# Modulation products of two 128-row blocks issued together, and seven raw tiles in place of four

## The chip, the core and the metric

The kernel runs on one core of a Trainium2 chip. Its engines work side by side: TensorE (PE; its weight loads are listed apart as PEld), VectorE (DVE), ScalarE (ACT), GpSimd (POOL) and SyncE (SP), which here only issues DMA transfers. The metric is device time in microseconds for one execution; the median of the runs counts, and less is better.

## The reference

Two layers of a trunk with 640 tokens of 1024 features (128 context tokens and 512 latent ones). Each layer has an FFN, a mixer and a second FFN. In front of each stands a norm with a shift and a scale, behind it a gate; the nine vectors of a layer come from the condition by one matrix product, the modulation, and this is what the change is about:

```
def adaln(cond, w, b):                       # w: (1024, 9 * 1024) for each layer
    m = (jax.nn.silu(cond) @ w + b).reshape(cond.shape[0], 1, N_MOD, D_MODEL)
    return [m[:, :, j] for j in range(N_MOD)]

for i in range(DEPTH):                       # DEPTH = 2; c_ctx for context, c for latent tokens
    m_ctx = adaln(c_ctx[None, :], mod_w[i], mod_b[i])
    m_lat = adaln(c, mod_w[i], mod_b[i])
    ...                                      # x += 1/2 gate * post(swiglu(pre(x) * (1 + scale) + shift)), and so on
```

Two condition vectors are multiplied with a matrix of 1024 x 9216 for each layer, 75 MB of weights in all, all in float32.

## The kernel before

**The modulation** is a generator, `adaln` (from L363 on). It works through groups (l, q): five for each layer, of 2048 columns each, the last of 1024. A group is the sum over eight blocks (`kc`) of 128 rows of the weights. For one block, `load` asks SP's DMA queue (L376) for two tiles `mw` of 128 x 1024 (one in the last group of a layer), and four matmuls follow (L393; two in a last group). The stationary operand is the 32-column `cT`, which holds the two conditions, the moving one 512 columns of weights; `tile_position=(0, 32 * j)` puts the four on four 32-column tiles of the array, so that they write four strips of one PSUM bank, `ad`. After each block the generator yields. At a group's end the bias `mb` is added (L399), and TensorE transposes the sum (L403).

**Who asks.** Outside, each call of `step()` or `filler()` runs the generator to its next yield: eight calls at the start, then one for each step `t` of an FFN (up to the number in `FILLS`), several at the end of an FFN behind its last products, and others between the pieces of the even mixer. With `self.look` set (in the mixer's scan and attention), a block's weights are asked for one call earlier.

**The raw tiles.** `raw()` gives one of four buffers of 128 x 1024 float32 (pool `rawp`), taken in turn as they come free. All weights land in them: the blocks `u` and `v` of an FFN step (L587) and the rows of its second matrix (L201), the mixers' projections (L196), the modulation's `mw` and `mb`, and the gates `gb`. A weight block is split in two parts by ScalarE and VectorE (`hi`, `lo`, L599 and L600), which frees its raw tile; an `mw` tile is read by TensorE itself, and its products free it.

**The FFN** forms its first product by seven products of halves (L646, 128 x 320 into `up`) and mixes them with pieces of the second (L298, 128 x 512 into `dn`). A step `t` handles 128 of 2816 hidden features. **The even mixer** projects (L208), runs a chunked scan (L1267 to L1287) and latent attention (keys and values from `ukv`, loaded at L1475 and first used at L1484; L1507 to L1580).

**What sets the order.** The code is written as one sequence; a scheduler gives each engine its own order of instructions from it, by their place in the sequence and by what they need. Each engine then works in that order. SP issues its transfers one after the other, and one that waits for a buffer holds up those behind it.

## Time and profile before

| | |
|---|---|
| median of 3 runs | 2749.08 us (2747.61 to 2754.76) |
| profiled execution, span from first to last instruction | 2748.3 us |
| TensorE, matmuls | 2671.1 us busy, 97% |
| TensorE, weight loads | 2335.4 us busy, 85% |
| VectorE | 1944.1 us busy, 71% |
| ScalarE | 1186.0 us busy, 43% |
| GpSimd | 125.5 us busy, 5% |
| DMA | 309.60 MB, mean 113 GB/s |

The profiled execution has no time of its own beside its span. An engine's busy share is a mean over stages. The matmuls are pipelined: one that is listed with 0.31 us may be followed by the next after 0.15, so what a matmul costs is read from one start to the next. The granted clock is given as a share of 2.4 GHz.

### The profile page before, as it was taken

How to read it: one execution, taken by the hardware profiler on the slowest of the kernel's cores; microseconds unless marked ns; L12 is line 12 of the kernel's file. 1: busy time of each engine (PE TensorE's matmuls, PEld its weight loads, DVE VectorE, ACT ScalarE, POOL GpSimd, SP SyncE). 2: the span in 40 equal slices, each digit the busy share in tenths (PEclk: the TensorE clock that was granted, in tenths of full speed). 3: DMA queues.
4: the chain of work that ended last, by engine and by line, in shares of the span. 5: the costliest groups of instructions: out<-in, count | busy, mean ns of one | idle time of the engine just before them, and what ended most of it. 6: DMA issues, size and time to landing. Idle time of an engine off the chain costs nothing.

```text
span 2748.3 us, 41207 instructions
## 1 busy us (share of the span) xinstructions
PE 2671.1 (97%) x16040; PEld 2335.4 (85%) x16040; DVE 1944.1 (71%) x3731; ACT 1186.0 (43%) x2285; POOL 125.5 (5%) x301
## 2 busy tenths in 40 slices
PE   6999999999999999999999999999999999999998
PEld 4888888788867678888997889999899988999997
DVE  5777677768575558667777777777775738777776
ACT  5433323555435556333335533333665446433333
POOL 0000000200100011000001000000200002000001
PEclk9999999999999999999999999999999999999999
DMA  7344333734141343434226432223312243322223
GB/s 251 116 125 142 124 115 106 236 113 124 57 157 57 118 161 116 129 115 131 77 70 195 131 96 84 85 70 112 125 43 73 64 133 115 93 85 85 74 80 123
DMA packets 297099, 309.60 MB, mean 113 GB/s; under 512 B 13573, under 2 KB 250639, under 8 KB 296903
## 3 DMA queue, kind: packets, MB, share of 16 engines
q1 hardware_dynamic: 278240, 260.05, 30.6%
q10 hardware_dynamic: 18663, 46.92, 4.9%
q8 instruction: 126, 2.06, 0.3%
q14 instruction: 70, 0.57, 0.1%
HBM read 286.59 MB, written 20.33 MB: 112 GB/s over the span
## 4 chain that ended last, share of the span: by engine, by line
PE 56%; issue 33%; DMA 3%; DVE 3%; ACT 2%; POOL 2%; POOLq 0%; DVEq 0%; ACTq 0%
PE up L646 18%; PE dn L298 13%; PE up L208 9%; PE ad L393 3%; PE up L1830 2%; PE dn L1810 1%; DMA mw<-in_mod_w_dram 1%; PE up L1542 1%; POOL rstd L231 1%; POOL ss L223 1%; POOL rstd L230 1%; DMA mb<-in_mod_b_dram 0%; DMA raw<-in_ffn_w_in_dram 0%; PE up L1575 0%; DMA cf<-const_cf_dram 0%
## 5 line engine op out<-in xcount | busy, mean ns | idle before, releaser
L646 PE MATMUL up<-ar,hi 128*128 128x320 f32 x2944 | 662.4, 313 | 8.6 <-ACT ar L509 3.9
L646 PEld LDWEIGHTS up<-ar,hi 128*128 128x128 f32 x2944 | 503.8, 189 | 40.5 <-ACT ar L509 5.5
L646 PE MATMUL up<-ar,lo 128*128 128x320 f32 x1472 | 457.0, 311 | 0.1
L599 ACT CAST hi<-raw 128x1024 fp32r<-128x1024 f32 x256 | 267.6, 1050 | 376.5 <-PE up L646 227.2
L600 DVE TENSOR_TENSOR lo<-raw,hi 128x1024 fp32r<-128x1024 f32 x256 | 312.6, 1222 | 89.6 <-ACT hi L599 88.9
L304 DVE TENSOR_TENSOR y<-y,dn 128x512 f32<-128x512 f32 x388 | 264.4, 683 | 147.7 <-PE dn L298 147.3
L298 PE MATMUL dn<-hi,al 128*128 128x512 f32 x880 | 347.1, 395 | 0.6 <-DVE al L687 0.6
L298 PE MATMUL dn<-hi,ah 128*128 128x512 f32 x880 | 346.7, 395 | 1.0 <-DVE y L304 0.9
L298 PE MATMUL dn<-lo,ah 128*128 128x512 f32 x880 | 347.5, 395 | 0.0
L646 PE MATMUL up<-hq,hi 128*128 128x320 f32 x1408 | 318.9, 312 | 0.0
L646 PEld LDWEIGHTS up<-ar,lo 128*128 128x128 f32 x1472 | 278.8, 189 | 1.7 <-issue 0.8
L646 PEld LDWEIGHTS up<-hq,hi 128*128 128x128 f32 x1408 | 238.4, 188 | 41.1 <-issue 22.6
L208 PE MATMUL up<-ar,hi 128*128 128x384 f32 (+1 forms) x1184 | 266.8, 315 | 4.5 <-ACT ar L274 3.7
L208 PEld LDWEIGHTS up<-ar,hi 128*128 128x128 f32 x1184 | 199.8, 190 | 21.2 <-issue 12.8
L646 PE MATMUL up<-hq,lo 128*128 128x320 f32 x704 | 217.5, 309 | 0.0
L183 DVE TENSOR_TENSOR lo<-raw,hi 128x1024 fp32r<-128x1024 f32 x145 | 176.0, 1219 | 51.0 <-ACT hi L182 47.2
L298 PEld LDWEIGHTS dn<-hi,al 128*128 128x128 f32 x880 | 165.4, 188 | 39.3 <-DVE al L687 1.3
L298 PEld LDWEIGHTS dn<-hi,ah 128*128 128x128 f32 x880 | 165.2, 188 | 25.2 <-DVE y L304 2.3
L208 PE MATMUL up<-ar,lo 128*128 128x384 f32 (+1 forms) x592 | 184.8, 312 | 0.0
L298 PEld LDWEIGHTS dn<-lo,ah 128*128 128x128 f32 x880 | 165.3, 188 | 22.4
L182 ACT CAST hi<-raw 128x1024 fp32r<-128x1024 f32 x145 | 151.3, 1048 | 42.4 <-PE up L646 15.1
L646 PE MATMUL up<-hq,hilo 128*128 128x320 f32 x960 | 155.5, 310 | 0.0
(704 smaller groups left out, 4139.3 us busy)
## 6 DMA issues: line engine op xcount, KB each, us to landing
raw<-in_ffn_w_in_dram SPq DMA_DIRECT2D x188, 512.0 KB
mw<-in_mod_w_dram SPq DMA_DIRECT2D x144, 512.0 KB
raw<-in_ffn_w_out_dram SPq DMA_DIRECT2D x88, 512.0 KB
xdr<-x ACTq DMA_DIRECT2D x25, 512.0 KB
x<-xdr ACTq DMA_DIRECT2D x25, 512.0 KB
raw<-in_od_w_in_dram SPq DMA_DIRECT2D x24, 512.0 KB
raw<-in_ev_w_in_dram SPq DMA_DIRECT2D x19, 512.0 KB
gb<-gate ACTq DMA_DIRECT2D x12, 512.0 KB
```

Source lines behind the costliest of these rows:

```text
L182: nc.scalar.copy(hi, raw)
L183: nc.vector.tensor_sub(lo, raw, hi.bitcast(F32))
L208: self.nc.tensor.matmul(ps[:, :n], lhsT=wt[a][:, kc], rhs=self.h[g][:, b, kc], start=k == 0, stop=k == 3 * KC - 1)
L223: nc.gpsimd.tensor_tensor(s2, tot, ss, ALU.add)
L230: nc.gpsimd.tensor_scalar(r, ss, 1.0 / D, EPS, ALU.mult, ALU.add)
L298: nc.tensor.matmul(ps, lhsT=a(i, m), rhs=w[j][:, nh * 512:nh * 512 + 512], start=k == 0, stop=k == last)
L304: nc.vector.tensor_add(yd, yd, ps)
L393: nc.tensor.matmul(ps[32 * j:32 * j + 32, :], lhsT=self.cT[:, kc], rhs=wt[j // 2][:, (j % 2) * 512:(j % 2) * 512 + 512], start=kc == 0, st ...
L599: nc.scalar.copy(hi, raw[:, :n])
L600: nc.vector.tensor_sub(lo, raw[:, :n], hi.bitcast(F32))
L646: nc.tensor.matmul(ps[:, :HT], lhsT=w[i][:, kc], rhs=b[j].at(kc), start=first and n == 0, stop=n == 11, skip_group_check=not first)
L1830: nc.tensor.matmul(ps[:, :256], lhsT=T.ht(a, kc, m), rhs=ws[kc // 4][b][:, kc % 4], start=k == 0, stop=k == 23)
```

## The change

Nothing is left out or added in what is computed. The code changes in three places; all docstrings and comments are gone too, and lines below L393 stand two to four lines further down (L646 is L650 after, L393 is L395).

```
-        self.rawp = mk("rawp", 4)
+        self.rawp = mk("rawp", 7)
...
                 ps = self.ps_ad.tile([P, 512], F32, tag="ad", name=self.u("ad"))
+                held = []
                 for kc in range(KC):
                     if not ready:
                         load()
-                    wt = ready.pop(0)
+                    held.append((kc, ready.pop(0)))
                     if self.look:
                         load()
-                    for j in range(nj):
-                        nc.tensor.matmul(ps[32 * j:32 * j + 32, :], lhsT=self.cT[:, kc], rhs=wt[j // 2][:, (j % 2) * 512:(j % 2) * 512 + 512], start=kc == 0, stop=kc == KC - 1, tile_position=(0, 32 * j))
+                    one = (l, q) == (0, 0)
+                    for k, wt, j in [(k, wt, j) for k, wt in held for j in range(nj)] if one or kc % 2 else []:
+                        nc.tensor.matmul(ps[32 * j:32 * j + 32, :], lhsT=self.cT[:, k], rhs=wt[j // 2][:, (j % 2) * 512:(j % 2) * 512 + 512], start=k == 0, stop=k == KC - 1, tile_position=(0, 32 * j))
+                    if one or kc % 2:
+                        held = []
                     if kc < KC - 1:
                         yield False
...
-    nc = bacc.Bacc("TRN2", target_bir_lowering=False, num_devices=1)
+    nc = bacc.Bacc("TRN2", target_bir_lowering=False, num_devices=1, dynamic_dma_scratch_size=1024)
```

In the first group the blocks' products are issued one block at a time, as before. In all others a call with even `kc` only asks for the block's weights and keeps them; the call with odd `kc` issues the products of both blocks. A kept block holds its raw tiles for one call longer. The pool of raw tiles grows by three, 12 KB in each partition, and the scratch space for DMA descriptors shrinks to make room.

Where the instructions stand is shown at three places. The first is TensorE's order in the first FFN, for the first two blocks of the second group of layer 0; `ad` is the modulation's bank, `mw` a weight tile with its number, `up` and `dn` the FFN's products. Before, the first block stands behind a piece of the second product:

```order
L298 MATMUL dn_2429<-lo_2266,ah_2237 128x512
L298 MATMUL dn_2429<-hi_2265,al_2238 128x512
L393 MATMUL ad_2457<-mw_2458,cT 32x512 x2
L393 MATMUL ad_2457<-mw_2460,cT 32x512 x2
L646 MATMUL up_2474<-hq_784,hi_2446 128x320
```

and the second block one step later, in two pieces:

```order
L646 MATMUL up_2496<-ar_403,lo_2447 128x320
L393 MATMUL ad_2457<-mw_2644,cT 32x512 x2
L646 MATMUL up_2660<-hq_784,hi_2621 128x320
L646 MATMUL up_2660<-hq_785,hi_2621 128x320
L646 MATMUL up_2660<-hq_784,lo_2622 128x320
L646 MATMUL up_2660<-hq_784,hi_2621 128x320
L646 MATMUL up_2660<-hq_785,hi_2621 128x320
L646 MATMUL up_2660<-hq_784,lo_2622 128x320
L646 MATMUL up_2660<-hq_784,hi_2621 128x320
L393 MATMUL ad_2457<-mw_2646,cT 32x512 x2
L646 MATMUL up_2660<-hq_785,hi_2621 128x320
```

After, at the place of the second block:

```order
L650 MATMUL up_2492<-ar_403,hi_2446 128x320 x2
L650 MATMUL up_2492<-ar_403,lo_2447 128x320
L395 MATMUL ad_2457<-mw_2458,cT 32x512 x2
L395 MATMUL ad_2457<-mw_2460,cT 32x512 x2
L395 MATMUL ad_2457<-mw_2640,cT 32x512 x2
L395 MATMUL ad_2457<-mw_2642,cT 32x512 x2
L650 MATMUL up_2660<-hq_784,hi_2617 128x320
L650 MATMUL up_2660<-hq_785,hi_2617 128x320
```

Both blocks now stand together, and the piece in the midst of `up_2660` is gone.

The second place is TensorE's order at the end of the second FFN, where the last group of layer 1 begins: `pt` is the transpose of the group before it, `up_13864` (`up_13862` after) the third FFN's first product. Before:

```order
L646 MATMUL up_13864<-ar_13350,lo_13500 128x320
L403 MATMUL pt_13710<-ident,mb_13707 128x128 x4
L393 MATMUL ad_13719<-mw_13720,cT 32x512 x2
L646 MATMUL up_13864<-ar_13350,hi_13499 128x320 x2
L646 MATMUL up_13864<-ar_13350,lo_13500 128x320
L393 MATMUL ad_13719<-mw_13724,cT 32x512 x2
L646 MATMUL up_13864<-ar_13350,hi_13499 128x320 x2
L646 MATMUL up_13864<-ar_13350,lo_13500 128x320
L646 MATMUL up_13864<-ar_13350,hi_13499 128x320 x2
L646 MATMUL up_13864<-ar_13350,lo_13500 128x320
L646 MATMUL up_13864<-ar_13350,hi_13499 128x320 x2
L646 MATMUL up_13864<-ar_13350,lo_13500 128x320
```

After:

```order
L650 MATMUL up_13862<-ar_13346,hi_13495 128x320
L650 MATMUL up_13862<-ar_13346,lo_13496 128x320
L407 MATMUL pt_13710<-ident,mb_13707 128x128 x4
L395 MATMUL ad_13719<-mw_13720,cT 32x512 x2
L395 MATMUL ad_13719<-mw_13722,cT 32x512 x2
L395 MATMUL ad_13719<-mw_13728,cT 32x512 x2
L395 MATMUL ad_13719<-mw_13730,cT 32x512 x2
L650 MATMUL up_13862<-ar_13346,hi_13495 128x320 x2
L650 MATMUL up_13862<-ar_13346,lo_13496 128x320
```

The first four blocks of that group, two products each, have moved together ahead of most of the first product.

The third place is SP's order in the even mixer's scan, around the load of `ukv`. Before:

```order
L376 DMA mw_7379<-in_mod_w_dram 128x1024
L376 DMA mw_7381<-in_mod_w_dram 128x1024
L376 DMA mw_7423<-in_mod_w_dram 128x1024
L1475 DMA ukv_7259<-in_ev_mla_w_ukv_dram 128x1024
L376 DMA mw_7425<-in_mod_w_dram 128x1024
L376 DMA mw_7468<-in_mod_w_dram 128x1024
```

After:

```order
L376 DMA mw_7375<-in_mod_w_dram 128x1024
L376 DMA mw_7377<-in_mod_w_dram 128x1024
L376 DMA mw_7423<-in_mod_w_dram 128x1024
L376 DMA mw_7425<-in_mod_w_dram 128x1024
L376 DMA mw_7464<-in_mod_w_dram 128x1024
L376 DMA mw_7466<-in_mod_w_dram 128x1024
L376 DMA mw_7525<-in_mod_w_dram 128x1024
L376 DMA mw_7527<-in_mod_w_dram 128x1024
L1479 DMA ukv_7259<-in_ev_mla_w_ukv_dram 128x1024
L376 DMA mw_7545<-in_mod_w_dram 128x1024
```

The `mw` tiles of the two blocks after 7425 now stand ahead of `ukv` too, four transfers more.

## Rows read from the trace of the kernel before

**Rows 1.** The page: busy shares; the chain that ended last, by engine and by line

```profile
PE 2671.1 (97%) x16040; PEld 2335.4 (85%) x16040; DVE 1944.1 (71%) x3731; ACT 1186.0 (43%) x2285; POOL 125.5 (5%) x301
...
PE 56%; issue 33%; DMA 3%; DVE 3%; ACT 2%; POOL 2%; POOLq 0%; DVEq 0%; ACTq 0%
PE up L646 18%; PE dn L298 13%; PE up L208 9%; PE ad L393 3%; PE up L1830 2%; PE dn L1810 1%; DMA mw<-in_mod_w_dram 1%; PE up L1542 1%; POOL rstd L231 1%; POOL ss L223 1%; POOL rstd L230 1%; DMA mb<-in_mod_b_dram 0%; DMA raw<-in_ffn_w_in_dram 0%; PE up L1575 0%; DMA cf<-const_cf_dram 0%
```

**Rows 2.** Windows of four stages: each engine's busy time, granted clock, DMA

```profile
core 0: us, PE busy (x) PEld busy (x) DVE busy (x) ACT busy (x) POOL busy (x), PEclk, DMA share, GB/s
45.00:425.00 380.00, 375.11 (x2187) 326.33 (x2188) 274.53 (x430) 140.76 (x213) 0.00 (x0) 0.99 0.41 128
...
680.00:1000.00 320.00, 313.65 (x2094) 235.15 (x2093) 189.67 (x647) 154.89 (x434) 15.71 (x18) 0.99 0.32 105
1060.00:1300.00 240.00, 240.00 (x1415) 211.00 (x1415) 175.74 (x274) 87.64 (x131) 0.00 (x0) 1.00 0.39 120
1480.00:1520.00 40.00, 33.45 (x161) 21.87 (x160) 26.43 (x60) 19.01 (x55) 8.70 (x21) 0.91 0.63 202
```

**Rows 3.** Timeline of TensorE, first FFN: start, duration, instruction, idle before

```profile
225.16 0.40 PE L298 MATMUL dn<-hi,al 128*128 128x512 f32 x1
225.49 1.06 PE L393 MATMUL ad<-mw,cT 128*32 128x512 f32 x8
226.49 0.56 PE L646 MATMUL up<-hq,hi 128*128 128x320 f32 x2
```

**Rows 4.** Timeline of TensorE, first FFN: a block in two halves

```profile
245.90 1.05 PE L393 MATMUL ad<-mw,cT 128*32 128x512 f32 x4
246.88 0.56 PE L646 MATMUL up<-hq,hi 128*128 128x320 f32 x2
...
247.86 0.31 PE L646 MATMUL up<-hq,hi 128*128 128x320 f32 x1
248.10 1.05 PE L393 MATMUL ad<-mw,cT 128*32 128x512 f32 x4
249.08 0.42 PE L646 MATMUL up<-hq,hi 128*128 128x320 f32 x1
```

**Rows 5.** Timelines of TensorE's matmuls and weight loads, even mixer

```profile
797.39 1.91 PE L393 MATMUL ad<-mw,cT 128*32 128x512 f32 x12
799.24 0.65 PE L1350 MATMUL pt<-ident,kq 128*128 128x128 f32 x4
...
797.39 0.16 PEld L393 LDWEIGHTS ad<-mw,cT 128*32 128x32 f32 x8 [0.54 <-issue]
```

**Rows 6.** Timeline of SP, first FFN; the chain's longest pieces

```profile
237.01 7.66 SPq L376 DMA_DIRECT2D mw<-in_mod_w_dram  x2
...
518.40 3.46 DMA mw<-in_mod_w_dram
```

**Rows 7.** Timelines of SP and TensorE in the scan; TensorE's waits, 680 to 1000 us

```profile
778.73 0.33 SPq L1475 DMA_DIRECT2D ukv<-in_ev_mla_w_ukv_dram  x1
...
775.33 1.06 PE L393 MATMUL ad<-mw,cT 128*32 128x512 f32 x6
...
PE up L1484 <- DMA ukv<-in_ev_mla_w_ukv_dram: 0.7, 1, 0.7
```

**Rows 8.** The modulation line's instructions: duration min, median, max in ns

```profile
L393 PEld LDWEIGHTS ad<-mw,cT x576: 105/108/157, 10.0 to 1604.5; 128*32 128x32 f32 x192
```

**Rows 9.** Timeline of TensorE, end of the second FFN

```profile
1498.29 0.85 PE L646 MATMUL up<-ar,hi 128*128 128x320 f32 x4 [1.66 <-ACT ar L509]
...
1502.10 0.63 PE L403 MATMUL pt<-ident,mb 128*128 128x128 f32 x4 [2.37 <-DVE ar L510]
1503.30 1.92 PE L393 MATMUL ad<-mw,cT 128*32 128x512 f32 x4 [0.58 <-DMA mw<-in_mod_w_dram]
1505.15 0.90 PE L646 MATMUL up<-ar,hi 128*128 128x320 f32 x2
...
1506.25 1.92 PE L393 MATMUL ad<-mw,cT 128*32 128x512 f32 x4
```

## The prediction

> **What bounds the kernel now.** I read the page first: TensorE is busy for 97% of a span of 2748.3 us, and in the chain that ended last its work holds the largest share [rows 1]. Then the stretches. From 45 to 425 us and from 1060 to 1300 us (the first and second FFN) TensorE is busy 375 of 380 and 240 of 240 us at a granted clock of 0.99 to 1.00, in the even mixer's scan and attention (680 to 1000 us) 314 of 320, while VectorE is busy 59 to 73% and the DMA engines 32 to 41% [rows 2]. So in nearly every stretch in which modulation products stand there is other TensorE work ready behind them, and a microsecond of TensorE removed is a microsecond of the span, unless something else becomes late. The exception is 1480 to 1520 us, where TensorE is busy 33 of 40 us at clock 0.91.
>
> Then what a modulation product costs its neighbours. I call a stretch of such products with nothing else between them a run. Each product (two records in the trace) fills one of four 32-column tiles of the array. A run of eight records, which is a whole 128-row block on all four tiles, goes from 225.49 us to the next ordinary product at 226.49: 1.00 us. Ahead of it lie 0.33 us from the start of the previous product, of which 0.21 is that product's own turn (512 columns at 2.4 GHz): 0.12 more [rows 3]. A run of four records, half a block on two tiles, takes 0.98 us at 245.90 and again at 248.10, with 0.11 ahead [rows 4]. So half a block costs what a whole one costs, 1.10 us: the tiles work at the same time, and a half leaves two of them idle. A run of twelve records, where tiles 0 and 1 have a second product, takes 1.85 us from 797.39 to 799.24 [rows 5]: a second round on the tiles costs 0.85 and not another 1.10. **Cost of a run: 0.25 us for going in and out, and 0.85 for each round** (the rounds are the products on its fullest tile).
>
> **The change, part by part.** The products themselves stay: 288 before and after, on the same tiles. What moves is where they stand. I counted runs and rounds in the order of instructions of both programs, leaving out the first eight blocks, whose order is unchanged. By stage, runs and rounds, then the cost by the formula: first FFN 23 and 23 to 8 and 16, 25.3 to 15.6 us; its end 10 and 11 to 7 and 9, 11.9 to 9.4; the even projection 14 and 14 to 6 and 12, 15.4 to 11.7; scan and attention 36 and 38 to 29 and 30, 41.3 to 32.8; second FFN 13 and 13 to 4 and 8, 14.3 to 7.8; its end 6 and 6 to 3 and 7, 6.6 to 6.7; third FFN 3 and 3 to 3 and 5, 3.3 to 5.0 (the last block of the second FFN has no partner until the stage end, and what follows shifts behind it). Together 105 runs with 108 rounds become 60 with 87. **Sum: 45 runs x 0.25 + 21 rounds x 0.85 = 11.3 + 17.9 = 29.1 us less TensorE time.** The scheduler cuts every second block of the FFN in two halves, which is where most of the lost rounds are; a pair goes four products wide, twice.
>
> No row shows the second round on tiles 2 and 3. On tiles 0 and 1 its weight loads are hidden: all eight loads of the run stand within 0.16 us at 797.39 [rows 5], though one takes 108 ns [rows 8], and the round costs 0.85 us, no more than its two passes of 512 columns (427 ns each at 2.4 GHz with four cycles a column). If the loads of each of the 24 added second to fourth rounds had to go one after the other, that would be 24 x 4 x 108 ns = 10 us and leave 19; if they are hidden, nothing. I take nothing, as rows 5 have it. The Trainium skill (TensorE: Matmul & The Clock Gate, Part 3, What overlaps and what doesn't) speaks against this change: it says that a weight load overlaps matmuls in flight only where it goes to other rows of the array, and these tiles all use the same rows; by that rule the saving would be the 19, and the run of twelve records disagrees with it.
>
> What is hidden. Holding the first block of a pair costs two raw tiles for one more step, which the three new ones pay. The DMA of a second block is the place to look: in the first FFN its two halves are issued at 237.01 and some 7.3 us later [rows 6], the second half 3.8 us ahead of its use at 248.10 [rows 4], and the chain has a block that took 3.46 us from issue to landing [rows 6]. The pair must have both halves at the place of 245.90. In the changed program the second half gets the tile that the u block of the step leaves, as the first half did before, or one that was left earlier; so it can be asked for by about 237.0, 8.9 us ahead, and nothing waits. Taken: 0. Without that cover: 244.3 + 3.5 - 245.9 = 1.9 us for each of the 12 FFN pairs, 23 us.
>
> SP's queue in the scan is the second such place. The load of ukv was issued at 778.73, its first product waited 0.7 us for it [rows 7], and now four more block loads stand ahead of it; the last of these needs a tile that the run at the place of 775.33 frees [rows 7]. That lets ukv be issued some 2 us after the start of that run (1 us of reading, three issues at 0.35), against 3.4 before, but with up to 1 MB more in flight ahead of it. Behind it on SP stand only later blocks and the z rows. Bounds: 0.7 us less (the wait is gone) to 4 more; taken: 0.
>
> The end of the second FFN waits already: 1.66 us for ScalarE, 2.37 for VectorE, then 0.58 for a modulation block, with two runs of four records whose rows read 1.92 us where the same run reads 1.05 at full clock [rows 4, 9]. After the change four half-wide blocks stand there as one run of four rounds, which waits for its last tile, freed by the run before. If that block lands like the one at 1503.3, the run takes 3.65 us at 2.4 GHz or about 7 at 1.2, against five runs of 1.85 + 1.85 + 3 x 0.98 = 6.6 and 0.6 of wait. Beyond what the sum already holds that is from 1.7 us less to 3.2 more; taken: 0. Elsewhere three more raw tiles let weights be asked for earlier; TensorE's longest wait for a weight is the one for ukv, so 0 again.
>
> The sum stays at 29 us, from 2748.3 to 2719. The median of the runs is 2749.1, 0.8 above that execution: **2720 us**.
>
> **The rivals.** (a) Attention doesn't pass its saving on. TensorE's work there is cut into short pieces behind ScalarE and VectorE; if shorter runs only uncover such waits, its 8.6 us go: 2729, and with 4 for ukv 2733. Against it: TensorE is busy 314 of 320 us there [rows 2]. (b) Only going in and out is saved, as if half-wide runs had cost half: 45 x 0.25 = 11 us, 2738. Rows 4 speak against it. Weight loads one after the other lie between, 2730. (c) **Slower: the pair waits for its second block.** In all 36 pairs the first block's products now also wait for the second's DMA, and TensorE, which takes matmuls in order, has nothing to put in front. If the second is still asked for when it was, each pair loses 1.9 us, 36 x 1.9 = 68 us: 2720 + 68 = 2788. It decides from 0.8 us for each pair on (29/36). For it: a load issued 3.8 us ahead of use [rows 4, 6]. Against it: the tiles of the changed program, above. (d) More than predicted: earlier requests also take away waits at the start and at both stage ends, some 9 us more: 2711. (e) The change does not do what it says, because the scheduler puts the pairs apart again: 2749; the order of instructions excludes it for the FFN, whose pairs stand together, and has it in part for attention, where 28 of 29 runs are one round, which the count holds already.
>
> The chances: forecast 0.74, with 2713 to 2726 as its own range; (a) 0.10; (b) or the weight loads 0.06; (c) 0.04; (d) 0.06; (e) nothing beyond the count. The range reaches from (d), 2711, to the worst of (a), 2733; outside it stay half of (b), (c), and some 0.08 for what I don't see in the reordered mixer. A measurement of this kernel tells about 0.3%, 8 us, from no change. Faster by that means under 2741: all but (c) give it, less something for the reordering; 0.92 faster, 0.05 the same, 0.03 slower.
>
> **What would show it.** In the first FFN the trace should have one run of sixteen records every other step, about 1.85 us from its first record to the next ordinary product; at 2.3 the weight loads don't overlap. The first FFN, the even mixer and the second FFN should be shorter by about 10, 12 and 6 us. VectorE's and ScalarE's busy time should stay. The prediction is wrong if TensorE waits for modulation blocks ahead of the sixteen-record runs (c), if the scan and attention have as much more idle TensorE time as the runs save (a), or if the run of four rounds waits longer than 3 us at the low clock.

## The result, and the profile after

The changed kernel takes 2712.97 us (median of 4 runs, 2711.59 to 2716.26), the kernel before beside it 2748.35 (4 runs): a ratio of 0.9875, 95% interval 0.9862 to 0.9887. The forecast was 2720 us, with a range of 2711 to 2733. The profiled spans, 2748.3 and 2714.5 us, are 33.8 apart. The page of the changed kernel, busy time, share and instructions of each engine:

```profile
span 2714.5 us, 41232 instructions
PE 2632.5 (97%) x16040; PEld 2331.2 (86%) x16040; DVE 1943.0 (72%) x3731; ACT 1179.1 (43%) x2281; POOL 125.5 (5%) x301
```

Beside [rows 1], TensorE is busy 38.6 us less with the same 16040 matmuls; VectorE's and ScalarE's busy time hardly changed (1.1 and 6.9 us less). The stretches that answer to [rows 2] (the later ones begin up to 30 us earlier), with each engine's busy time, the granted clock and the DMA:

```profile
45.00:425.00 380.00, 374.83 (x2246) 337.47 (x2247) 282.37 (x448) 144.93 (x218) 0.00 (x0) 0.99 0.41 130
1048.00:1288.00 240.00, 239.94 (x1437) 216.49 (x1436) 177.60 (x269) 86.85 (x127) 0.00 (x0) 1.00 0.36 117
666.00:983.00 317.00, 309.47 (x2121) 238.30 (x2120) 191.74 (x640) 152.23 (x417) 16.59 (x20) 0.99 0.33 115
1450.00:1490.00 40.00, 37.59 (x203) 27.38 (x203) 34.66 (x76) 26.12 (x73) 9.87 (x24) 0.96 0.75 256
```

In the same 380 us the first FFN now gets through 2246 matmuls where it got through 2187. At the end of the second FFN, TensorE is busy 37.6 of 40 us (33.5 before) at clock 0.96 (0.91 before).

A pair in the first FFN, TensorE and then its weight loads, at the place of [rows 3, 4]:

```profile
240.84 0.31 PE L650 MATMUL up<-ar,lo 128*128 128x320 f32 x1
241.08 1.92 PE L395 MATMUL ad<-mw,cT 128*32 128x512 f32 x16
242.93 0.56 PE L650 MATMUL up<-hq,hi 128*128 128x320 f32 x2
...
241.08 0.16 PEld L395 LDWEIGHTS ad<-mw,cT 128*32 128x32 f32 x8 [0.19 <-issue]
241.53 0.13 PEld L395 LDWEIGHTS ad<-mw,cT 128*32 128x32 f32 x4 [0.30 <-issue]
241.96 0.13 PEld L395 LDWEIGHTS ad<-mw,cT 128*32 128x32 f32 x4 [0.30 <-issue]
```

Sixteen records take 1.85 us to the next ordinary product, and the second block's loads lie inside that time. TensorE's waits from 666 to 983 us no longer name ukv [rows 7].

**Where the time went.** Of all TensorE products that are not modulation products there are 15464 in each trace, in the same order by stage. The table gives the time from one of them to another, the same two in every kernel (numbers 200, 2400, 2800, 3600, 5400, 7600, 8400 and 9000; in the kernel before they start at 71.8, 474.4, 558.5, 692.3, 988.2, 1392.1, 1543.5 and 1648.5 us). Behind the stroke stands what the runs in that stretch cost: for each run, the time from the start of the product ahead to the start of the one behind, less that product's own turn. A wait that falls at a run is therefore in its cost. x1 to x12 are the experiments below, one profiled execution each. Where TensorE never waits, kernels with the same order agree within 0.2 us (the first FFN of x1, x3, x9 and x10); the stretch behind the third FFN, alike in all fourteen, lies between 1088 and 1094 us to the last product.

| kernel | first FFN | its end | projection | scan, attention | second FFN | its end | third FFN | runs in all |
|---|---|---|---|---|---|---|---|---|
| before | 402.6 / 25.5 | 84.1 / 12.5 | 133.8 / 15.2 | 296.0 / 43.6 | 403.9 / 15.3 | 151.4 / 11.6 | 105.0 / 3.3 | 127.0 |
| changed | 391.0 / 15.7 | 84.5 / 9.6 | 130.2 / 11.6 | 288.6 / 35.8 | 397.1 / 7.9 | 146.1 / 11.9 | 105.4 / 3.9 | 96.3 |
| x1 | 386.9 / 17.7 | 83.3 / 10.1 | 133.0 / 13.0 | 287.6 / 37.2 | 399.5 / 9.9 | 145.0 / 6.8 | 104.9 / 3.3 | 97.9 |
| x2 | 409.2 / 33.6 | 84.3 / 12.8 | 133.9 / 12.8 | 302.9 / 50.4 | 408.2 / 9.6 | 153.8 / 13.6 | 106.9 / 3.9 | 136.6 |
| x3 | 387.1 / 17.7 | 85.1 / 8.9 | 133.0 / 13.0 | 285.9 / 29.7 | 397.8 / 9.9 | 147.3 / 5.7 | 104.7 / 3.3 | 88.2 |
| x4 | 401.0 / 17.4 | 109.7 / 28.6 | 146.9 / 27.6 | 301.3 / 10.3 | 401.5 / 11.8 | 150.9 / 11.8 | 106.4 / 4.4 | 111.8 |
| x5 | 389.1 / 15.7 | 83.2 / 8.6 | 130.2 / 11.6 | 290.4 / 30.6 | 396.6 / 7.9 | 151.1 / 5.6 | 105.3 / 3.9 | 83.9 |
| x6 | 393.2 / 15.9 | 84.5 / 9.4 | 130.2 / 11.6 | 289.1 / 27.6 | 395.9 / 7.9 | 144.7 / 9.0 | 105.3 / 3.9 | 85.3 |
| x7 | 388.9 / 15.8 | 87.5 / 12.1 | 130.3 / 11.6 | 303.2 / 47.1 | 394.9 / 7.9 | 146.0 / 11.4 | 105.4 / 3.9 | 110.0 |
| x8 | 390.1 / 17.7 | 86.8 / 11.3 | 133.2 / 13.0 | 308.7 / 52.7 | 401.6 / 9.9 | 148.8 / 8.9 | 104.9 / 3.3 | 116.7 |
| x9 | 386.9 / 17.7 | 83.4 / 9.9 | 130.2 / 11.6 | 289.9 / 36.8 | 397.6 / 7.9 | 146.1 / 11.9 | 105.4 / 3.9 | 99.7 |
| x10 | 386.9 / 17.7 | 83.4 / 9.7 | 130.2 / 11.6 | 288.3 / 34.5 | 394.9 / 7.9 | 151.0 / 9.2 | 105.5 / 3.9 | 94.4 |
| x11 | 384.6 / 15.7 | 83.1 / 9.4 | 131.3 / 11.6 | 288.0 / 35.5 | 394.8 / 7.9 | 152.1 / 9.1 | 105.5 / 3.9 | 93.1 |
| x12 | 389.1 / 15.7 | 84.2 / 9.9 | 129.4 / 10.7 | 278.9 / 9.6 | 394.4 / 7.0 | 145.6 / 11.1 | 105.4 / 3.9 | 67.9 |

From before to changed the runs cost 127.0 - 96.3 = 30.7 us less. By stage the time fell by 11.6, -0.4, 3.6, 7.4, 6.8, 5.3 and -0.4 us; behind the third FFN, where no run stands, both kernels take 1090 us to the last product.

Two things lie behind these times that the runs do not show: TensorE's idle time, and its granted clock. In some stretches the clock stands at 0.5, the lower of its two levels (1.2 in place of 2.4 GHz); an estimate of what such a stretch costs, at most, is half its length. Two lines show it, the scan and attention of the changed kernel and then of x5:

```profile
677.90:966.40 288.50, 280.97 (x1961) 214.39 (x1960) 174.11 (x614) 144.20 (x397) 15.71 (x18) 0.99 0.31 109
676.50:967.00 290.50, 281.89 (x1963) 217.63 (x1962) 173.84 (x614) 145.13 (x399) 15.72 (x18) 0.96 0.32 109
```

Idle time of TensorE, then half of the time at 0.5, in us, from the same traces:

| stage | before | changed | x1 | x2 | x3 | x4 | x5 | x6 | x7 | x8 | x9 | x10 | x11 | x12 |
|---|---|---|---|---|---|---|---|---|---|---|---|---|---|---|
| scan, attention: idle | 6.3 | 7.5 | 6.3 | 10.3 | 8.5 | 25.4 | 8.6 | 12.3 | 8.4 | 13.8 | 5.9 | 6.5 | 7.1 | 14.1 |
| clock | 3.4 | 1.7 | 1.7 | 4.7 | 5.1 | 18.8 | 11.9 | 8.5 | 6.8 | 13.7 | 5.1 | 6.8 | 3.4 | 8.5 |
| end of second FFN: idle | 7.0 | 3.3 | 4.5 | 8.9 | 6.5 | 8.0 | 8.6 | 4.2 | 1.8 | 7.1 | 3.3 | 8.7 | 10.1 | 3.2 |
| clock | 3.4 | 1.7 | 0.0 | 3.4 | 1.7 | 3.4 | 5.1 | 0.0 | 0.0 | 1.7 | 1.7 | 1.7 | 1.7 | 1.7 |

The clock is no accident of the one traced execution: its mean over the whole span was 0.991 to 0.993 in the four timed executions of the changed kernel and 0.988 to 0.990 in those of x5.

### The profile page after: what moved, and what is told of

It reads as the page before. It is cut to its first block, busy times and chain, and to the rows that moved or that the text cites. A ratio compares the mean times of both kernels' runs of the same rounds, so it can differ in the third digit from the quotient of the medians.

```text
span 2714.5 us, 41232 instructions
## 1 busy us (share of the span) xinstructions
PE 2632.5 (97%) x16040; PEld 2331.2 (86%) x16040; DVE 1943.0 (72%) x3731; ACT 1179.1 (43%) x2281; POOL 125.5 (5%) x301
## 5 line engine op out<-in xcount | busy, mean ns | idle before, releaser
L650 PE MATMUL up<-ar,hi 128*128 128x320 f32 x2944 | 658.6, 311 | 10.5 <-ACT ar L513 4.5
L650 PEld LDWEIGHTS up<-ar,hi 128*128 128x128 f32 x2944 | 502.4, 189 | 37.2 <-ACT ar L513 6.1
L650 PE MATMUL up<-ar,lo 128*128 128x320 f32 x1472 | 455.5, 310 | 0.6 <-DVE lo L604 0.6
L650 PE MATMUL up<-hq,hi 128*128 128x320 f32 x1408 | 315.1, 310 | 0.3 <-DVE xn L707 0.3
L650 PEld LDWEIGHTS up<-ar,lo 128*128 128x128 f32 x1472 | 277.9, 189 | 1.3 <-DVE lo L604 1.3
L650 PEld LDWEIGHTS up<-hq,hi 128*128 128x128 f32 x1408 | 238.8, 188 | 21.5 <-issue 9.2
L650 PE MATMUL up<-hq,lo 128*128 128x320 f32 x704 | 217.4, 309 | 0.0
L208 PEld LDWEIGHTS up<-ar,hi 128*128 128x128 f32 x1184 | 200.6, 191 | 15.3 <-issue 5.6
L182 ACT CAST hi<-raw 128x1024 fp32r<-128x1024 f32 x145 | 150.9, 1048 | 44.5 <-PE up L208 19.0
L658 ACT COPY h<-up 128x320 f32<-128x320 f32 x68 | 29.0, 426 | 314.3 <-PE up L650 314.3
```

The lines of the kernel that those rows point to most:

```text
L182: nc.scalar.copy(hi, raw)
L208: self.nc.tensor.matmul(ps[:, :n], lhsT=wt[a][:, kc], rhs=self.h[g][:, b, kc], start=k == 0, stop=k == 3 * KC - 1)
L650: nc.tensor.matmul(ps[:, :HT], lhsT=w[i][:, kc], rhs=b[j].at(kc), start=first and n == 0, stop=n == 11, skip_group_check=not first)
L658: self.T.nc.scalar.copy(p1, X[:, :HT])
```

## The experiments

Ratios are to the kernel before, timed beside each, with the 95% interval; kernels of different sets are compared by them.

**x1: the raw tiles alone.** The seven tiles and the smaller scratch stay as in the changed kernel, the pairs go:

```diff
-                    one = (l, q) == (0, 0)
+                    one = True
```

> Seven raw tiles (and the smaller scratch), but the products of each block issued at its own request, as before. In the program's order this has 79 runs with 86 rounds behind the first eight blocks, against 105 with 108 before and 60 with 87 in the changed kernel: with seven tiles the two halves of a block mostly stay together. Theory (0.25 us per run and 0.85 us per round, however the rounds come about): 26 x 0.25 + 22 x 0.85 = 25 us below the kernel before, 2723 us, and 2717 if the 6 us that the changed kernel gained beyond the sum came with the earlier requests; then pairing itself is worth 4 us and the tiles the rest. Rival (the pairs carry the gain, the tiles only make room for them): 2740 to 2748 us.

Measured: 2715.07 us, ratio 0.9867 (0.9853 to 0.9880). The changed kernel's 0.9875 lies inside that interval: **the tiles alone give the whole gain, and the pairs add nothing that can be measured.** The rival is out, and the theory's 4 us for the pairs as well. That it is the tiles and not the smaller scratch is shown by x8, which has the same scratch, no pairs and five tiles, and no gain. The runs show how. In the first FFN every block now goes in one run:

```profile
222.30 0.40 PE L298 MATMUL dn<-hi,al 128*128 128x512 f32 x1
222.63 1.06 PE L395 MATMUL ad<-mw,cT 128*32 128x512 f32 x8
223.63 0.56 PE L650 MATMUL up<-hq,hi 128*128 128x320 f32 x2
```

The halves of [rows 4] are gone without any pair, and the runs there fall from 25.5 to 17.7 us. Pairing takes off the last 2.0 (15.7), yet the first FFN of the changed kernel is 4.1 us longer than that of x1. The four transposes at the end of a group of eight blocks hold the reason. Timelines of VectorE and TensorE in the changed kernel:

```profile
245.04 0.69 DVE L403 TENSOR_TENSOR mb<-mb,ad 128x512 f32<-128x512 f32 x1 [1.66 <-DMA mb<-in_mod_b_dram]
...
245.78 0.66 PE L407 MATMUL pt<-ident,mb 128*128 128x128 f32 x4 [1.27 <-DVE mb L403]
```

VectorE waits for the bias row, TensorE for VectorE. The kernel before waits at the same two groups of the first FFN, 3.6 us in all (3.2 in the changed kernel, nothing listed in x1): the tiles take this wait away, and the pairs bring it back. The instruction that asks for the row, by its tile (duration in ns, start in us), in the changed kernel:

```profile
L402 ACTq DMA_DIRECT2D mb<-in_mod_b_dram x1: 582/582/582, 239.5 to 239.5; - x1
```

So the row is used 5.5 us after it was asked for. The same instruction in x1:

```profile
L402 ACTq DMA_DIRECT2D mb<-in_mod_b_dram x1: 583/583/583, 223.8 to 223.8; - x1
```

There the row was asked for 16 us earlier, and the transposes follow the products without a gap, as x1's timeline has it:

```profile
245.89 0.31 PE L650 MATMUL up<-hq,hilo 128*128 128x320 f32 x1
246.04 0.60 PE L407 MATMUL pt<-ident,mb 128*128 128x128 f32 x4
```

The bias too lives in a raw tile, and a held pair has four of them; that this is why it was asked for late is argued here and tried in x6 and x11.

**x2: the pairs alone.**

```diff
-        self.rawp = mk("rawp", 7)
+        self.rawp = mk("rawp", 4)
```

> The products of two blocks issued together as in the changed kernel, but from four raw tiles. In the program's order: 90 runs with 107 rounds (the pairs come apart again into halves, in the first FFN above all: 24 runs with 24 rounds there), against 105 with 108 before. Theory (runs and rounds): 15 x 0.25 + 1 x 0.85 = 4.6 us below the kernel before, 2744 us, or more if TensorE waits for the requests that the held tiles put off. Rival (pairing carries the gain): 2715 to 2725 us.

Measured: 2774.11 us, ratio 1.0079 (1.0066 to 1.0092): slower, and neither number. The count (4.6 us less) says nothing of waits, and they are what came; TensorE's (in all, times, longest), in the first FFN and then from 1000 to 1480 us:

```profile
PE ad L395 <- DMA mw<-in_mod_w_dram: 6.5, 10, 1.7
PE pt L407 <- DVE mb L403: 2.8, 2, 1.5
...
PE pt L407 <- DVE mb L403: 5.4, 1, 5.4
...
PE dn L298 <- ACT hi L182: 3.6, 1, 3.6
```

Ten runs in the first FFN waited for their blocks: this is the prediction's rival (c), and the added tiles are what keeps it away.

**x3: one by one, the half that lands last first.** As x1, and in the loop of the products:

```diff
-... for j in range(nj)]
+... for j in range(nj)[::-1]]
```

> Seven raw tiles, block by block, and within a block the four products in reverse, the half that lands last first, so that all four are ready when the first of them is. In the program's order: 68 runs with 74 rounds, no block split in the FFNs, 22 runs in scan and attention. Theory (runs and rounds): 37 x 0.25 + 34 x 0.85 = 38 us below the kernel before, 2710 us, and 2704 with the 6 us beyond the sum: faster than the changed kernel without any pair. Rival (a pair is needed, as in and out is what costs): 74 rounds' saving would not show, and 68 runs against 60 would be slower than the changed kernel, 2715 us or more. Second rival: the run waits on TensorE for its last half, 0.3 us or more each, 2730 us.

Measured: 2714.01 us, ratio 0.9861 (0.9846 to 0.9876), no different from x1, though its runs cost 9.7 us less (88.2 against 97.9). That is the theory's 38 us below the kernel before, but by luck: x1, to which the count gives 25, is as low, and the 13 us between the two did not come. In scan and attention the runs fall by 7.5 us against x1 and the stage by 1.7: idle time grows by 2.2 and the part of the clock by 3.4. At the end of the first and second FFN the runs fall by 1.2 and 1.1 and the stages get 1.8 and 2.3 longer. No pair is needed, so the first rival is out too.

**x4: pairs kept whole.** The order within a pair is turned (block and half that land last first, start and stop with them), and the eight products are put ahead of up to 2000 instructions traced before them:

```diff
-                    for k, wt, j in [(k, wt, j) for k, wt in held for j in range(nj)] ...
+                    with self.ahead(2000):
+                        for k, wt, j in [(k, wt, j) for k, wt in held[::-1] for j in range(nj)[::-1]] ...
```

> Seven raw tiles and pairs, the block that landed last first and its last half first, and the eight products issued ahead of what was traced up to 2000 instructions before them, so that the scheduler does not take them apart in scan and attention. In the program's order: 36 runs with 72 rounds, 7 with 14 of them in scan and attention (29 with 30 in the changed kernel). Theory (runs and rounds): 69 x 0.25 + 36 x 0.85 = 48 us below the kernel before, 2700 us, and 2694 with the 6 us beyond the sum. Rival (a pair in the middle of attention holds up the chain there by more than its separate halves did, which sat in idle time or cost nothing): 2710 to 2720 us. Second rival (TensorE waits for the second block's transfer, since the pair is put as early as it can go): above 2720 us.

Measured: 2793.55 us, ratio 1.0151 (1.0137 to 1.0165): slower; the second rival's waits are there. TensorE's over the whole span:

```profile
PE ad L396 <- DMA mw<-in_mod_w_dram: 35.2, 20, 5.7
```

The changed kernel has three such waits there, 4.7 us. In the projection the runs cost 27.6 us in place of 11.6; waits for blocks (5.1 us) and one of 4.7 for the bias are 9.8 of these 16. In scan and attention they cost only 10.3, and the stage is longer than before: TensorE is idle for 25.4 us there, and the time at half clock counts for 18.8 more (7.5 and 1.7 in the changed kernel). So the first rival, a pair that holds up the chain, is not excluded for that stage.

**x5: the turned pairs without being put ahead.** The edit of x4 without its `with` line.

> The changed kernel, with the products of a pair in reverse: the block that landed last first and its last half first, so that a pair or block is not taken apart. In the program's order 47 runs with 74 rounds (the changed kernel 60 with 87, the blocks one by one with the last half first 68 with 74). Theory A (the count of runs and rounds passes on whole): 14 us below the changed kernel, 2699 us. Theory B (it passes on in the FFNs and the projection, where TensorE has other work behind it; in scan and attention most of it turns into waits for VectorE and ScalarE, as in the run before with the last half first, which saved 7.5 us of runs there and lost 5.7 in waits): in FFNs and projection the count is that of the changed kernel, so 2710 to 2714 us.

Measured: 2719.65 us, ratio 0.9894 (0.9881 to 0.9908): both theories missed, A by 21 us. Runs cost 12.4 us less than in the changed kernel (83.9 against 96.3) and the time is longer. The FFNs and the projection are as theory B has them. Scan and attention save 5.2 us of runs and get 1.8 longer. It is not waits that eat the saving, as theory B has it: idle time grows by 1.1 us, and the part of the clock by 10.2 (1.7 to 11.9). The end of the second FFN gets 5.0 longer; from 1380 to 1560 us TensorE's first wait is

```profile
PE pt L257 <- ACT ar L513: 6.3, 1, 6.3
```

the chain that prepares the next sub-layer's tokens, which a shorter run does not hasten.

**x6: the bias earlier.** x5, and the bias's tile and its load moved from behind the last block to

```diff
                 for kc in range(KC):
+                    if kc == KC - 2:
+                        mb = self.raw("mb")
+                        ...
```

> The run before it in this set (pairs, last block and half first) with one more edit: the raw tile of the bias is taken and its row asked for two requests earlier, ahead of the last pair. In the changed kernel VectorE waited 1.66 us for that row at 245 us, and TensorE 1.27 us for VectorE, ahead of the four transposes; the same stands at 411 us (2.2 us between starts), while with the blocks one by one no such wait stands there. Theory: the transposes in the first FFN come without a wait, 3 us less than the run before it, 2708 to 2711 us. Rival (the bias takes the tile that the next block would have had, and the wait only moves to the next pair): no difference from the run before it.

Measured: 2721.19 us, ratio 0.9900 (0.9887 to 0.9914). The rival is right in the result: the wait for the bias is gone from the first FFN, and others stand in its place, though not at the next pair. TensorE's waits there, then VectorE's for a weight block (longest 6.2 us, 0.9 in x5):

```profile
PE up L651 <- DVE xn L716: 4.4, 2, 2.3
PE ad L399 <- DMA mw<-in_mod_w_dram: 0.2, 1, 0.2
...
DVE s L621 <- DMA raw<-in_ffn_w_in_dram: 13.3, 5, 6.2
```

The first FFN takes 393.2 us, 4.1 more than x5. That TensorE's 4.4 us come from that block is argued.

**x7: tile by tile.**

```diff
-... [(k, wt, j) for k, wt in held for j in range(nj)] ...
+... [(k, wt, j) for j in range(nj) for k, wt in held] ...
```

> The changed kernel, with the eight products of a pair tile by tile: both blocks' products of tile 0, then both of tile 1, and so on, so that neighbours lie on the same tile. The products and their number are the same. Theory (a round is what lies on different tiles next to each other; a second product on the same tile can only begin when the first is through): a pair in the FFN takes 0.25 + 5 x 0.85 = 4.5 us where it took 1.96; in the program's order 58 runs with 171 rounds, 0.85 x 84 = 71 us more than the changed kernel, 39 of them in the FFNs and the projection, where they pass on whole: 2752 to 2784 us. Rival (the tiles have queues of their own, so that products of other tiles go past the one that waits): 2713 us, as the changed kernel.

Measured: 2735.28 us, ratio 0.9956 (0.9943 to 0.9969). The theory is wrong where it was sure: a pair in the FFN, whose products now stand in the order 0, 0, 1, 1, 2, 2, 3, 3, takes what it took.

```profile
240.80 0.31 PE L650 MATMUL up<-ar,lo 128*128 128x320 f32 x1
241.04 1.94 PE L395 MATMUL ad<-mw,cT 128*32 128x512 f32 x16
242.92 0.41 PE L650 MATMUL up<-hq,hi 128*128 128x320 f32 x1
```

That is 1.88 us where alternating tiles take 1.85. So a product waits for its own tile and not for those ahead of it, and the rounds of a run are the products on its fullest tile, in whatever order, as the prediction defined them; the expectation's 171 counted neighbours. By the fullest tile x7 has 58 runs with 104 rounds, 17 rounds and 14 us more than the changed kernel, and its runs cost 110.0 - 96.3 = 13.7 us more. Of these, 11 rounds and 11.3 us come in scan and attention, where the scheduler takes the pairs apart between tiles, and the stage is 14.6 us longer: what goes on top of it is paid in full, and the clock's part grows with it (1.7 to 6.8).

**x8: five tiles, one by one.** x1 with `mk("rawp", 5)`.

> Five raw tiles in place of seven, the products block by block as before the change. In the program's order 88 runs with 92 rounds: the blocks of the FFNs and the projection are whole as with seven tiles, those of scan and attention are mostly in halves (35 runs there; with seven 29, with four 36). Theory (the gain of the tiles is that blocks stay whole): 18 us below the kernel before by the count, 2730 us, down to 2722 with what the seven tiles gave beyond the count. Rival (the gain comes from weights asked for earlier, for which seven are needed): 2738 us or more.

Measured: 2747.79 us, ratio 0.9995 (0.9986 to 1.0004): no gain, as the rival has it, and yet the first FFN is 12.5 us shorter with its blocks whole, as the theory has it. Scan and attention give the gain back (308.7 us, 12.7 more than before): against the kernel before, TensorE is idle 7.5 us longer there, and the clock's part is 10.3 us larger. TensorE's longest wait of that stage:

```profile
PE ad L395 <- DVE mb L403: 5.4, 1, 5.4
```

The instructions on the bias tile there:

```profile
L402 ACTq DMA_DIRECT2D mb<-in_mod_b_dram x1: 581/581/581, 786.3 to 786.3; - x1
L403 DVE TENSOR_TENSOR mb<-mb,ad x1: 687/687/687, 796.0 to 796.0; 128x512 f32<-128x512 f32 x1
```

The bias again: asked for at 786.3 and added at 796.0; until then the next group's first product cannot have the one PSUM bank of the modulators (the pool `ps_ad` has one buffer). With seven tiles the same row was asked for at 747.0 (x1) and 750.3 (changed kernel) and added 13 us later without that wait. Five tiles keep the FFNs' blocks whole; the rest of the gain needs more of them. How much of the lost clock follows from this one wait is not shown.

**x9: the first FFN one by one, pairs behind it.**

```diff
-                    one = (l, q) == (0, 0)
+                    one = l == 0 and q < 3
```

> The changed kernel, but the blocks of the first FFN (two groups of eight) issued one by one, all later ones in pairs. In the program's order 68 runs with 87 rounds (60 with 87 in the changed kernel; all eight added runs in the first FFN, 2 us of going in and out). Theory: what the pairs lose in the first FFN is the wait for the bias row at the end of each group, which stands in the changed kernel (TensorE's products from 106 to 474 us of the kernel before took 359.1 us there) and not with the blocks one by one (353.9); so 5 us less than the changed kernel, 2708 us. Rival (the wait comes from the later order as well and comes back here): 2713 to 2715 us.

Measured: 2710.94 us, ratio 0.9864 (0.9850 to 0.9879). In the stretch of the expectation it takes 353.9 us, the theory's number to the tenth, and the wait for the bias is gone. The whole is the lowest median of the kernels that compute everything, 2 us below the changed kernel (3 by the ratios) where 5 were forecast; the intervals overlap, so that it beats it is not shown. (Its row in the table is from the slowest of its four executions, 2716.35 us.)

**x10: an eighth tile for x9.** `mk("rawp", 8)`, and the scratch cut from 1024 to 128.

> The run before it in this set with an eighth raw tile (the scratch cut again to make room). In the program's order 64 runs with 84 rounds: 2.2 us less by the count in scan and attention, 1.3 elsewhere. Theory A (raw tiles are what is short): at least these 3.5 us below the run before it, about 2704 us. Theory B (in scan and attention the count turns into waits for VectorE and ScalarE): the same as the run before it, 2706 to 2710 us.

Measured: 2714.76 us, ratio 0.9872 (0.9858 to 0.9887): nothing more. Scan and attention save 2.3 us of runs and 1.6 of time against x9, the second FFN 2.7, and the end of the second FFN takes 4.9 more, with 5.4 us more of idle TensorE.

**x11: eight tiles, pairs, the bias early.** The changed kernel with the edits of x6 (the bias) and x10.

> The changed kernel with an eighth raw tile and the bias row asked for two requests earlier, the pairs in their old order. With seven tiles the early bias took the wait ahead of the transposes away and brought another: TensorE waited 4.4 us in the first FFN for sums that waited for a weight block, since the bias held the tile the weight would have had. Theory: with the eighth tile neither wait stands there; the first FFN (106 to 474 us of the kernel before) takes 353 to 355 us where the changed kernel took 359.1 and the early bias with seven tiles 361.2; the whole 2706 to 2709 us. Rival (the wait for the weight has another cause than the tile): the first FFN stays at 359 to 361 us, 2712 us or more.

Measured: 2716.60 us, ratio 0.9880 (0.9864 to 0.9897). In the first FFN the theory holds: no wait of TensorE from 90 to 465 us is listed at all, and the stretch of the expectation takes 352.6 us, the shortest of all. With a tile more, the same early bias makes no product wait there; that the tile alone is what x6 lacked is likely, but not shown, since x6 also has the pairs turned. The total is missed at the end of the second FFN (152.1 us, 6.0 more than the changed kernel). All engines' waits from 1455 to 1500 us:

```profile
ACT f L239 <- DVE f L241: 9.6, 4, 6.8
DVE s L621 <- DMA raw<-in_ffn_w_in_dram: 5.5, 1, 5.5
...
PE pt L257 <- ACT ar L514: 5.2, 1, 5.2
```

VectorE waited 5.5 us for a weight block, and TensorE 5.2 us for ScalarE. The same two waits stand at that end in x5 (4.4 and 6.3 us) and x10 (3.9 and 3.6), whose ends take 151.1 and 151.0 us, and neither in the changed kernel and x9 (146.1 each); x1 has them shorter (3.5 and 1.5 us, 145.0). That the one causes the other is argued.

**x12: most products of scan and attention left out.**

```diff
-... for j in range(nj)] ...
+... for j in range(nj) if l == 0 or q > 2 or k in (0, KC - 1)] ...
```

> The changed kernel without most of the products that stand in scan and attention: of the second layer's first three groups only the first and the last block are multiplied (the blocks are still fetched), so those modulators are wrong. In the program's order the runs of scan and attention fall from 29 with 30 rounds to 6 with 6, 32.8 to 6.6 us by the count; 1.6 us go elsewhere. It bounds from below what any order of the products could make of that stage. Theory A (a run there costs TensorE's full time): 28 us below the changed kernel, 2685 us. Theory B (most of what the runs take there would be waiting for VectorE and ScalarE without them; the run with the last half first gave back 5.7 of 7.5 us): 8 us or less from that stage, 2703 to 2707 us.

Measured: 2706.80 us, ratio 0.9841 (0.9828 to 0.9855); the profiled execution took 2700.5. The total is theory B's: the runs of the stage fall by 26.2 us (35.8 to 9.6) and the stage by 9.7. The stage without most runs, beside the changed kernel's third window above:

```profile
666.00:975.00 309.00, 294.88 (x1988) 239.90 (x1987) 192.98 (x645) 151.03 (x417) 17.43 (x21) 0.97 0.35 114
```

TensorE is idle 14 us in place of 7.5, and its granted clock is 0.97 in place of 0.99: some 6.6 us, and 2% of 309 or 6 us, of the 16.5 that the stage did not give. So the waits of theory B are less than half of it.

## Why the prediction was right, and where not

- **What a run costs: right.** By the formula a pair costs 0.25 + 2 x 0.85 = 1.95 us. The eight in the first FFN of the changed kernel cost 1.96 each. The forecast saving of 29.1 us stands against 30.7. That half-wide runs cost as much as whole ones is seen in x1 and x8, whose first FFN saved 7.8 us of runs by not halving blocks. Rivals (b) and (e) are out.
- **The weight loads: right.** One takes 109 ns at the median, and all of the second round lie behind the first. The prediction misread its row, though: the run of twelve has twelve loads and not eight, and the last four stand further on, beside the products ahead of them (kernel before):

```profile
797.85 0.12 PEld L393 LDWEIGHTS ad<-mw,cT 128*32 128x32 f32 x2 [0.30 <-issue]
798.28 0.12 PEld L393 LDWEIGHTS ad<-mw,cT 128*32 128x32 f32 x2 [0.31 <-issue]
```

  So a whole round has eight loads, and the prediction's 10 us for loads one after the other were too low, by up to half. The rule of the Trainium skill (TensorE: Matmul & The Clock Gate, Part 3, What overlaps and what doesn't), that loads overlap only where the rows differ, would have made the pair 0.4 us longer by the prediction's four loads, 0.9 by eight; the trace disagrees with it, 1.85 us as forecast.
- **No wait for the second block: right.** The first FFN, projection and second FFN of the changed kernel have no wait for a modulation block. That the three tiles pay for it is shown by x2 (ten waits, 6.5 us, in the first FFN alone).
- **What carries the gain: this step failed.** The prediction took the tiles as the price of holding a pair and set their own worth at 0 ("three more raw tiles let weights be asked for earlier ... so 0 again"). Rival (d) gives earlier requests 9 us on top of the pairs; none has the tiles carry the gain. x1 has the gain without a pair, x2 has a loss with pairs and no tiles. In x1 the runs cost 29.1 us less than before, and 7.9 more come in the first FFN outside them, 5.6 of these around the two places where the kernel before waits for the bias. The sum came out right because it was counted from the order of the whole changed program, in which the tiles had already put the halves together. Pairing itself takes 2.0 us of runs off each FFN and 1.4 off the projection, and in the first FFN loses about 6 us outside the runs (375.3 us against 369.2 in x1). Product by product, 5.1 us of that stand around the two waits for the bias: 3.2 of waiting, and 1.7 for products behind the second wait, where the clock is at its lower level. The rest is a wait for a row of norms (0.9) and one for VectorE (0.6), less small differences.
- **The FFNs and the projection pass it on: right.** Forecast -9.7, -3.7, -6.5; measured -11.6, -3.6, -6.8. Of the first, 9.8 are runs.
- **End of the first FFN: wrong by 3 us.** Forecast -2.5, measured +0.4: the runs fell by 2.9, and the rest of the stage took 74.9 us in place of 71.6; TensorE was idle for 4.8 us there in place of 2.0.
- **Scan and attention: right in size (-8.6 forecast, -7.4 measured), but less safe than it looked.** "TensorE is busy 314 of 320 us" was read as "a microsecond of TensorE is a microsecond of the span". For what x3, x5 and x12 took away beyond the changed kernel, 6.1, 5.2 and 26.2 us of runs, the stage gave 2.7, -1.8 and 9.7. Rival (a), waits for ScalarE and VectorE, is only a part of that: idle time grew by 1.0, 1.1 and 6.6 us, and the clock's part by 3.4, 10.2 and 6.8. The prediction read the clock of this stage (0.99) and did not ask what shorter runs would make of it.
- **End of the second FFN: the size was off.** Forecast 0, between 1.7 less and 3.2 more beyond the sum; measured -5.3 us. The run of four rounds came as foreseen and took 5.25 us, between the 3.65 and 7 given for the two clocks. Of the bounds, 1.7 comes out of the terms named there (7.2 to 3.65, less the 1.85 that the formula holds for five runs made one); 3.2 does not, since 7.2 to 7 gives 1.65:

```profile
1470.94 0.81 PE L650 MATMUL up<-ar,hi 128*128 128x320 f32 x3 [2.29 <-ACT ar L513]
1471.58 0.31 PE L650 MATMUL up<-ar,lo 128*128 128x320 f32 x1
1472.02 0.63 PE L407 MATMUL pt<-ident,mb 128*128 128x128 f32 x4
1472.58 5.32 PE L395 MATMUL ad<-mw,cT 128*32 128x512 f32 x16
1477.83 0.56 PE L650 MATMUL up<-ar,hi 128*128 128x320 f32 x2
```

  What was not foreseen: the waits of 2.37 for VectorE and 0.58 for a block [rows 9] are gone, and one of 2.29 stands where 1.66 stood. In all, TensorE's idle time there fell from 7.0 to 3.3 us and the clock's part from 3.4 to 1.7, which is the 5.3. Between kernels this stage lies anywhere from 144.7 to 153.8 us; why the order of one kernel meets that chain well and another's badly was followed only as far as x11 has it.

## What to carry to other kernels

Count what a change does to the program's order, but then ask of each part of it whether it alone gives that order: here a buffer count did the work that the rearranged products were written for. A count of TensorE time is good where TensorE always has something behind it; in a stage that alternates with other engines it held for the first 8 us and not for the next 26, and there the granted clock has to be read beside the waits, since it took as much as they did or more. In a pool shared by large and small loads, look first at the small one that is asked for last: in eight of the fourteen kernels here a row of biases held TensorE up for 2 us or more.

## What the runs showed of the hardware

- Products on different 32-column tiles do not wait for each other even when they stand in line: with neighbours on the same tile sixteen records take 1.88 us, with alternating tiles 1.85 (x7). The Trainium skill (TensorE: Matmul & The Clock Gate, Part 3, What overlaps and what doesn't) says that matmuls start and end strictly in the program's order; by that, a product on tile 1 would wait behind both on tile 0, which x7 does not show.
- A bias row of 256 KB can take longer than a weight tile of 512 KB. In the chain of the kernel before, one weight tile took 3.46 us from issue to landing [rows 6], two bias rows 5.63 and 6.05. In x8 a row was added 9.7 us after its issue, and VectorE waited for it.
- A wait can cost TensorE more than its length. In the changed kernel its 1.92 us wait for VectorE ended at 410.99; from 411.5 to 414.5 us the granted clock was 0.50, and products of 128 x 320 started 0.27 us apart, where the same products in x1, without the wait and at clock 1.00, started 0.15 apart. In all, the products behind the wait took 1.7 us longer than in x1:

```profile
410.99 0.74 PE L407 MATMUL pt<-ident,mb 128*128 128x128 f32 x4 [1.92 <-DVE mb L403]
411.40 0.86 PE L650 MATMUL up<-hq,hi 128*128 128x320 f32 x2
412.06 0.47 PE L650 MATMUL up<-hq,lo 128*128 128x320 f32 x1
```
